# A depthwise convolution on GpSimd by two phases of tokens: 47 half-width taps in place of 62

## The chip, the cores and the metric

The kernel runs on one NeuronCore of a Trainium2 chip. TensorE (PE) multiplies matrices, VectorE (DVE), ScalarE (ACT) and GpSimd (POOL) work elementwise, and SyncE (SP) issues the DMAs between HBM and the on-chip memory SBUF. Every engine executes its own list of instructions in order; an instruction whose operands are not ready holds up everything behind it in its list. TensorE writes to PSUM, eight banks of 128x512 fp32 numbers. The metric is the device time of one execution in microseconds (us). Times are given as the median of several runs; the profile belongs to one more execution.

## The reference

One layer of a streaming encoder over 1088 tokens (1024 of a prompt, 64 of a sample), model width 1024, fp32:

```python
h = x + 0.5 * _swiglu(x, ffn1_norm, ffn1_w_in, ffn1_w_out)
u = _rms(h, mix_norm)
z = u @ w_in                      # q | k | v | q_idx | k_idx | w_idx | conv GLU in | gates
...                               # rotary, indexer scores, top-k keys per query, attention over them
c = ca * jax.nn.sigmoid(cb)
c_pad = jnp.concatenate([past_conv, c], axis=1)
dc = lax.conv_general_dilated(c_pad, conv_w[:, None, :], window_strides=(1,), padding='VALID',
                              feature_group_count=CONV_CH) + conv_b      # 31 taps, 512 channels
conv_out = jax.nn.silu(_layernorm(dc, conv_ln_g, conv_ln_b)) @ conv_w_out
g_a, g_c = jnp.split(jax.nn.sigmoid(gate + b_gate), 2, axis=-1)
merged = g_a * (attn @ attn_w_out) + g_c * conv_out
h = h + merged @ w_out
h = h + 0.5 * _swiglu(h, ffn2_norm, ffn2_w_in, ffn2_w_out)
```

The change concerns `dc` alone: every channel is filtered over time with its own 31 coefficients. With channels on the partitions, one tile of 128 channels is a row of 1148 numbers per partition (30 of padding, 1024 of the prompt, 30 of the sample's past, 64 of the sample), and it gives 1118 sums, output n being the bias plus the sum over j of w[j] * c[n + j].

## The kernel before

Activations stand channels by tokens; every large product is made of three fp32r matmuls (high and low parts of weights and activations), so a weight is loaded by SP as `raw`, rounded by ACT to `whi` (L118) and its rest `wlo` is made by POOL (L119). `raw` and `whi`/`wlo` have three buffers each. The order of every engine's list comes from a scheduler that simulates the program with its own costs and priorities; nothing is reordered at run time.

The stages are: feed-forward 1, the input projection with the convolution and the indexer (790 to 1204 us of the profile), attention with what is left of gates, convolution branch and merge (to about 1650 us), the output projection, feed-forward 2. In the stage that the change touches these things run side by side:

- **Projections on PE**, in chunks of 364 or 362 tokens. A chunk of one weight is 24 matmuls into one of four PSUM banks (`ps4`): conv GLU columns for tiles 0 and 3, keys, indexer queries, values, conv GLU columns for tiles 1 and 2 (`conv_in`), attention queries, and then twelve of the sixteen gate weights (`gates`, three chunks each). ACT takes each gate chunk out of PSUM with a Tanh into `sg` (L1138), and SP stores it (L1139).
- **The convolution** (`conv`). Tile 3 goes to DVE (L751). Tiles 0, 1 and 2 go to ACT and POOL: a tile is done in two halves of 559 outputs; ACT makes the first product with the bias (`ac`, L761) and then for each of 30 further taps a product `pd` = w[j] * c (L765); POOL adds it to `ac` (L766). There are two buffers of `pd`, so ACT can be two taps ahead of POOL, and one buffer each of the input `ci` and of `ac`. A half ends with the store of `ac` (L767).
- **The indexer and its top-k**: scores by PE (L919, L920), Relu on ACT (L921), weighted sums `Y` on DVE (L924, L926), a POOL memset of the causal corner (L929), and then a search of the 256th largest score per row: 15 rounds of counting (L989 on DVE, L979 on ACT for one tile), the low bits (L1018, L1020), the mask `bias` (L1054), and behind a branch on a value read by DVE the breaking of ties (L1106 to L1115), tile by tile in the order 5, 6, 4, 3, 2, 1, 0 with a flag tested for each.
- **The start of attention**: logits `lg` (L1185, L1186) into three new PSUM banks that lie over those of `ps4` and so wait until every gate chunk is out of them; DVE adds `bias` to `lg` (L1188), which waits for the whole search; ACT exponentiates (L1198). The other four gates and the layer norm of the convolution's output (`norm`, from L1274) are filled in between.

Of the kernel before, what the change touches and what calls it, by code (L numbers as in the profile page):

```python
# [9 lines left out]
F32 = mybir.dt.float32  # L10
# [5 lines left out]
AF = mybir.ActivationFunctionType  # L16
ALU = mybir.AluOpType
AX = mybir.AxisListType

P = 128  # L20
# [34 lines left out]
CW = 31  # L55
# [3 lines left out]
PAR = {}  # L59
# [33 lines left out]
class Kern:  # L93
# [349 lines left out]
    def ffn(self, h, s, offs, gp, tp, steps, tail, lead=(), ready=(), last=False, lp=None):  # L443
# [20 lines left out]
        if lead:  # L464
            run(ready)
# [60 lines left out]
    def run(self):  # L526
        tc, nc, a = self.tc, self.nc, self.a
        PS = bass.MemoryType.PSUM
        with ExitStack() as top:
# [6 lines left out]
            d_c = dram.tile([4, P, 1148], F32, name="d_c")  # L536
            d_dc = dram.tile([4, P, 1118], F32, name="d_dc")
# [12 lines left out]
            for n_, o_, w_ in (("bgate", 0, 16), ("lnb", 16, 4)):  # L550
                q0 = PAR[n_][0]
                nc.scalar.activation(hb[:, o_:o_ + w_], self.par[:, q0:q0 + w_], AF.Copy, scale=0.5)
            wq = cst.tile([P, 9, 8], F32, name="wq")

            def par(n, i=0):
                o = PAR[n][0] + i
                return self.par[:, o:o + 1]
# [175 lines left out]
            bias = bp.tile([P, BCOLS], BF16, name="bias")  # L733
            cvs = ExitStack()
            cvp_ = self.pool(cvs, "convp", 1, side="right")
            ep = self.pool(cvs, "evict", 1, side="right")
            low = ExitStack()
            kp = self.pool(low, "topk", 1, side="right")
# [2 lines left out]
            def conv(t, dve):  # L741
                x = "d" if dve else "p"
                if dve:
                    for s0, w in ((0, 374), (374, 372), (746, 372)):
                        ci = cvp_.tile([P, 589], F32, name="ci", tag="ci" + x)[:, :w + 30]
                        nc.sync.dma_start(ci, d_c[t, :, s0:s0 + w + 30])
                        ac = lgi.tile([P, 512], F32, name="acc", tag="lgi")[:, :w]
                        nc.scalar.activation(ac, ci[:, 0:w], AF.Identity, scale=par("convw", t * CW),
                                             bias=par("convb", t))
                        for j in range(1, CW):  # L750
                            nc.vector.scalar_tensor_tensor(ac, ci[:, j:j + w], par("convw", t * CW + j), ac,  # L751
                                                           op0=ALU.mult, op1=ALU.add)
                        co = cvp_.tile([P, 559], F32, name="ac", tag="ac" + x)[:, :w]
                        nc.scalar.activation(co, ac, AF.Copy)
                        nc.sync.dma_start(d_dc[t, :, s0:s0 + w], co)
                    return
                for s0 in (0, 559):
                    ci = cvp_.tile([P, 589], F32, name="ci", tag="ci" + x)
                    nc.sync.dma_start(ci, d_c[t, :, s0:s0 + 589])
                    ac = cvp_.tile([P, 559], F32, name="ac", tag="ac" + x)  # L760
                    nc.scalar.activation(ac, ci[:, 0:559], AF.Identity, scale=par("convw", t * CW),  # L761
                                         bias=par("convb", t))
                    for j in range(1, CW):
                        pd = cvp_.tile([P, 559], F32, name="pd", tag="pd", bufs=2)
                        nc.scalar.activation(pd, ci[:, j:j + 559], AF.Copy, scale=par("convw", t * CW + j))  # L765
                        nc.gpsimd.tensor_tensor(ac, ac, pd, op=ALU.add)  # L766
                    nc.sync.dma_start(d_dc[t, :, s0:s0 + 559], ac)  # L767

            def load_q(pool, src, t0, rows, qpool=None, qb=2, n=1280):

# [18 lines left out]

            conv_in(3, ep)  # L790
            conv(0, False)
            conv(3, True)
            tbs = ExitStack()
            kx = self.pool(tbs, "kidx", 1)
# [37 lines left out]
            for i in (0, 1):  # L832
                b = bias[:, BOFF[i]:BOFF[i] + ATILES[i][3]]
# [20 lines left out]
            def spare(n):  # L854
                rows, y0, L = rows_of(n)
                return bias[:rows, BOFF[n + 2]:BOFF[n + 2] + L]
# [51 lines left out]
            for n in SORD:  # L908
# [4 lines left out]
                for hd in range(8):  # L913
                    nb = 2 if L > 512 else 1
                    pw = L // nb
                    for b in range(nb):
                        o = lgi.tile([P, 512], F32, name="lgi", tag="lgi")[:rows, :pw]
# [33 lines left out]
            r2s.close()  # L951
            conv_in(1, ep)
            conv(1, False)
            conv_in(2, ep)
            conv(2, False)
# [102 lines left out]
            with tc.If(more > 0):  # L1058
# [40 lines left out]
                for n in (5, 6, 4, 3, 2, 1, 0):  # L1099
# [4 lines left out]
                    with tc.If(tied > 0):  # L1104
                        y, b = Y[:rows, y0:y0 + L], spare(n)
# [280 lines left out]
            def gate_part():  # L1386
                steps = gates(gorder[GPRE:], ak, 2)
                for _ in range(3 * (16 - GPRE) - 7):
                    next(steps)
                    yield  # L1390
                lp = C["pool"] = self.pool(cx, "ln", 1)
                yield from both(norm(2, lp, lp), steps)
                act_es.close()

            def conv_part():
                lp_ = C["pool"]
                with cx:
                    lq = self.pool(cx, "lnq", 1, side="right")
                    for c, q in ((2, lq), (1, lp_), (0, None)):
                        yield from both(conv_out(c, lq), norm(c - 1, lp_, q) if c else iter(()))  # L1400

            def merge_part():
                self.act = self.pool(ac_es, "act2", 2, side="right")
                self.mp = self.pool(mg_es, "merge", 1, side="right")
                yield from merge(2, self.mp)

            def wout_part():
                yield from wout(2, h_dram(self.mp))

            def last_part():  # L1410
                yield from merge(1, self.mp)
# [8 lines left out]
            parts = [gate_part(), conv_part(), merge_part(), wout_part(), last_part()]  # L1420
# [211 lines left out]
```

## Time and profile before

| | us |
|---|---|
| median of 3 runs | 2360.64 (2358.08 to 2363.79) |
| the profiled execution | 2364.21, its span 2362.4 |
| PE busy | 2254.3 (95% of the span) |
| POOL busy | 1557.9 (66%) |
| DVE busy | 1690.9 (72%) |
| ACT busy | 1416.6 (60%) |

Shares of the span are averages over stages with different limits. How to read what is shown below: a row of the timeline is start, duration, engine, source line, operation, output tile<-input tiles, shapes, count, and in brackets how long the engine was idle before it and what released it. A row of waits is the waiting instruction and what it waited for, with the total in us, the number of times and the longest. A row of the windows is a stretch of time, its length, and for PE, PEld (weight loads), DVE, ACT and POOL the busy time and the number of instructions, then the granted clock of TensorE (1.00 is full), the DMA share and GB/s.

### The profile page before, as it was taken

The page shows a single profiled execution, that of the slowest core. Times are in us where ns is not written, and L with a number is a line of the kernel's source. Part 1 is how long each engine was busy: PE and PEld are TensorE (multiplying, and loading weights), DVE is VectorE, ACT ScalarE, POOL GpSimd, SP SyncE. Part 2 cuts the span into 40 slices and gives each one's busy share as a digit, 9 for nine tenths or more (in the row PEclk, how much of TensorE's full clock was granted, in tenths as well). Part 3 has the DMA queues.
Part 4 walks back from the last instruction along what each step waited for, and adds up shares of the span by engine and source line. Part 5 has one row for each costly group of instructions (what it writes and reads, how often), then busy time and mean ns, then how long its engine had stood idle before and what let it go on. Part 6 is the DMA issues. An engine that isn't in the chain of part 4 may idle for free. (4 is left out here: it accounts for less than half of the span.)

```text
span 2362.4 us, 44344 instructions
## 1 busy us (share of the span) xinstructions
PE 2254.3 (95%) x16226; PEld 2216.6 (94%) x16226; DVE 1690.9 (72%) x3868; ACT 1416.6 (60%) x2926; POOL 1557.9 (66%) x1071
## 2 busy tenths in 40 slices
PE   7999999999999999999979998899999999999997
PEld 6999998999999999999978888799999999999997
DVE  7887766887767287689846777457877757887765
ACT  6655655656646546887456667447655555556553
POOL 5667755767657786889863544558667765667654
PEclk9999999999999999999989999999999999999999
DMA  5332323333334434234222446763333232333333
GB/s 187 107 107 91 108 93 116 99 99 99 99 99 135 138 127 135 85 105 134 85 84 73 149 143 180 224 214 108 99 99 102 88 121 68 110 112 103 99 99 110
DMA packets 130412, 273.45 MB, mean 116 GB/s; under 512 B 17936, under 2 KB 77200, under 8 KB 130192
## 3 DMA queue, kind: packets, MB, share of 16 engines
q1 hardware_dynamic: 130192, 270.61, 35.8%
q8 instruction: 127, 2.08, 0.4%
q14 instruction: 93, 0.76, 0.1%
HBM read 231.87 MB, written 38.75 MB: 115 GB/s over the span
## 5 line engine op out<-in xcount | busy, mean ns | idle before, releaser
L136 PE MATMUL ps<-x,wp 128*128 128x272 f32 x1760 | 508.5, 290 | 6.3 <-ACT wp L152 3.3
L138 PE MATMUL ps<-x,wp 128*128 128x272 f32 x1760 | 504.3, 291 | 4.4 <-POOL wp L153 2.6
L137 PE MATMUL ps<-x,wp 128*128 128x272 f32 x1760 | 506.5, 289 | 0.0
L136 PE MATMUL ps<-x,whi 128*128 128x272 f32 (+2 forms) x1544 | 482.6, 313 | 10.5 <-ACT sg L1138 3.6
L153 POOL TENSOR_TENSOR wp<-s,wp 128x512 fp32r<-128x512 f32 x272 | 363.9, 1349 | 190.0 <-ACT wp L152 185.9
L138 PE MATMUL ps<-x,wlo 128*128 128x272 f32 (+2 forms) x1544 | 480.8, 312 | 0.0
L327 POOL TENSOR_TENSOR wlo<-raw,whi 128x1024 fp32r<-128x1024 f32 x120 | 290.4, 2420 | 186.7 <-ACT whi L326 177.8
L137 PE MATMUL ps<-x,whi 128*128 128x272 f32 (+2 forms) x1334 | 412.1, 309 | 1.0 <-POOL x L153 1.0
L119 POOL TENSOR_TENSOR wlo<-raw,whi 128x1024 fp32r<-128x1024 f32 (+1 forms) x123 | 277.9, 2262 | 154.0 <-ACT whi L118 149.1
L136 PEld LDWEIGHTS ps<-x,wp 128*128 128x128 f32 x1760 | 331.3, 189 | 10.6 <-ACT wp L152 4.7
L138 PEld LDWEIGHTS ps<-x,wp 128*128 128x128 f32 x1760 | 328.5, 188 | 8.2 <-DVE wp L153 4.4
L137 PEld LDWEIGHTS ps<-x,wp 128*128 128x128 f32 x1760 | 332.0, 189 | 0.0
L136 PEld LDWEIGHTS ps<-x,whi 128*128 128x128 f32 x1544 | 292.8, 190 | 13.4 <-ACT sg L1138 3.9
L766 POOL TENSOR_TENSOR ac<-ac,pd 128x559 f32<-128x559 f32 x180 | 272.5, 1514 | 39.6 <-ACT ac L761 19.0
L138 PEld LDWEIGHTS ps<-x,wlo 128*128 128x128 f32 x1544 | 292.7, 190 | 1.0
L137 PEld LDWEIGHTS ps<-x,whi 128*128 128x128 f32 x1334 | 253.6, 190 | 2.3 <-POOL x L153 1.3
L152 ACT ACTIVATE wp<-s 128x512 fp32r<-128x512 f32 x272 | 167.8, 626 | 130.3 <-DVE s L314 80.6
L765 ACT ACTIVATE pd<-ci,par 128x559 f32<-128x559 f32 x180 | 135.7, 758 | 96.8 <-POOL ac L766 85.8
L152 ACT ACTIVATE wp<-ps 128x512 fp32r<-128x512 f32 x208 | 123.1, 592 | 113.1 <-DVE ps L312 100.2
L439 DVE SCALAR_TENSOR_TENSOR h<-ps,h 128x272 f32<-128x272 f32 x448 | 174.9, 431 | 13.1 <-PE ps L138 12.4
L326 ACT ACTIVATE whi<-raw 128x512 fp32r<-128x512 f32 x240 | 138.5, 624 | 74.5 <-DMA raw<-wf 70.4
L137 PE MATMUL ps<-gl,whi 128*128 128x272 f32 x640 | 182.7, 291 | 0.0
(278 smaller groups left out, 5934.0 us busy)
## 6 DMA issues: line engine op xcount, KB each, us to landing
raw<-wf SPq DMA_DIRECT2D x353, 512.0 KB, 3.4
d_g<-sg SPq DMA_DIRECT2D x32, 181.0 KB, 1.9
d_h<-h SPq DMA_DIRECT2D x2, 2176.0 KB, 10.3
y<-t SPq DMA_DIRECT2D x32, 136.0 KB, 1.8
raw<-wf SPq DMA_DIRECT2D x16, 256.0 KB, 2.7
raw<-d_q SPq DMA_DIRECT2D x32, 128.0 KB, 3.0
raw<-d_qi SPq DMA_DIRECT2D x24, 128.0 KB, 3.2
d_g<-sg SPq DMA_DIRECT2D x16, 182.0 KB, 2.9
```

The source lines that it names most:

```text
L119: self.weng.tensor_tensor(lo[:, :n], raw[:, :n], hi[:, :n], op=ALU.subtract)
L136: t.matmul(out, wh, xh, start=first, stop=False, skip_group_check=onto)
L137: t.matmul(out, wh, xl, start=False, stop=False, skip_group_check=onto)
L138: t.matmul(out, wl, xh, start=False, stop=last, skip_group_check=onto)
L152: nc.scalar.activation(hi, x, AF.Copy)
L153: (eng or nc.vector).tensor_tensor(lo, x, hi, op=ALU.subtract)
L326: self.nc.scalar.activation(hi[:, c], raw[:, c], AF.Copy)
L327: self.weng.tensor_tensor(lo, raw, hi, op=ALU.subtract)
L439: nc.vector.scalar_tensor_tensor(x, p, 0.5, x, op0=ALU.mult, op1=ALU.add)
L765: nc.scalar.activation(pd, ci[:, j:j + 559], AF.Copy, scale=par("convw", t * CW + j))
L766: nc.gpsimd.tensor_tensor(ac, ac, pd, op=ALU.add)
```

## The change

In place of two halves of 559 neighbouring outputs, a tile on ACT and POOL is now cut into even and odd outputs. The whole row of 1148 inputs is loaded at once; `even` and `odd` are views of it with every second number, and `both` (tile `cb`) is a POOL addition of the two, shifted. Three filters of half width run over them, with the 15 odd coefficients over `odd`, the 16 even ones over `even`, and 16 sums of neighbouring coefficients over `both` (`cvs2`, made once). With o, e and w their results, the even outputs are e + o and the odd ones w - o - e shifted by one; the biases (once in o, twice in w) come out right. So a tile has 15 + 16 + 16 = 47 products in place of 62, 44 additions of products in place of 60, and four further additions (one for `both`, three for the outputs, two of which write every second number). Two thirds of the products read every second fp32 number. The input row and the output row share two buffers (tag `cip`), `ac` has three, `pd` two as before. A tile is loaded by one DMA and stored by one, in place of two and two. DVE's tile is unchanged.

```diff
@@ run()
             cvp_ = self.pool(cvs, "convp", 1, side="right")
+            cvs2 = cvp_.tile([P, 4, 17], F32, name="cvs2")
+            q0 = PAR["convw"][0]
+            w31 = self.par[:, q0:q0 + 4 * CW].rearrange("p (t j) -> p t j", j=CW)
+            q0 = PAR["convb"][0]
+            nc.gpsimd.tensor_tensor(cvs2[:, :, 0:15], w31[:, :, 0:30:2], w31[:, :, 1:31:2], op=ALU.add)
+            nc.scalar.activation(cvs2[:, :, 15], w31[:, :, 30], AF.Copy)
+            nc.scalar.activation(cvs2[:, :, 16], self.par[:, q0:q0 + 4], AF.Copy, scale=2.0)
@@ conv(t, dve), the branch for ACT and POOL
-                for s0 in (0, 559):
-                    ci = cvp_.tile([P, 589], F32, name="ci", tag="ci" + x)
-                    nc.sync.dma_start(ci, d_c[t, :, s0:s0 + 589])
-                    ac = cvp_.tile([P, 559], F32, name="ac", tag="ac" + x)
-                    nc.scalar.activation(ac, ci[:, 0:559], AF.Identity, scale=par("convw", t * CW),
-                                         bias=par("convb", t))
-                    for j in range(1, CW):
-                        pd = cvp_.tile([P, 559], F32, name="pd", tag="pd", bufs=2)
-                        nc.scalar.activation(pd, ci[:, j:j + 559], AF.Copy, scale=par("convw", t * CW + j))
+                ci = cvp_.tile([P, 1150], F32, name="ci", tag="cip", bufs=2)
+                nc.sync.dma_start(ci[:, 0:1148], d_c[t])
+                nc.gpsimd.memset(ci[:, 1148:1150], 0.0)
+                even, odd = (ci.rearrange("p (m t) -> p m t", t=2)[:, :, i] for i in (0, 1))
+                both = cvp_.tile([P, 574], F32, name="cb", tag="cb")
+                nc.gpsimd.tensor_tensor(both, even[:, 1:575], odd[:, 0:574], op=ALU.add)
+                q0 = PAR["convw"][0] + t * CW
+                parts = ((odd, 559, par("convb", t), [self.par[:, q0 + 2 * i + 1:q0 + 2 * i + 2] for i in range(15)]),
+                         (even, 560, None, [self.par[:, q0 + 2 * i:q0 + 2 * i + 1] for i in range(16)]),
+                         (both, 559, cvs2[:, t, 16:17], [cvs2[:, t, i:i + 1] for i in range(16)]))
+                sums = []
+                for x, n, b, ws in parts:
+                    ac = cvp_.tile([P, 560], F32, name="ac", tag="acp", bufs=3)[:, :n]
+                    sums.append(ac)
+                    if b is None:
+                        nc.scalar.activation(ac, x[:, 0:n], AF.Copy, scale=ws[0])
+                    else:
+                        nc.scalar.activation(ac, x[:, 0:n], AF.Identity, scale=ws[0], bias=b)
+                    for j in range(1, len(ws)):
+                        pd = cvp_.tile([P, 560], F32, name="pd", tag="pd", bufs=2)[:, :n]
+                        nc.scalar.activation(pd, x[:, j:j + n], AF.Copy, scale=ws[j])
                         nc.gpsimd.tensor_tensor(ac, ac, pd, op=ALU.add)
-                    nc.sync.dma_start(d_dc[t, :, s0:s0 + 559], ac)
+                o, e, w_ = sums
+                out = cvp_.tile([P, 1150], F32, name="co", tag="cip", bufs=2)
+                oe, oo = (out[:, 0:1118].rearrange("p (m t) -> p m t", t=2)[:, :, i] for i in (0, 1))
+                nc.gpsimd.tensor_tensor(oe, e[:, 0:559], o, op=ALU.add)
+                nc.gpsimd.tensor_tensor(w_, w_, o, op=ALU.subtract)
+                nc.gpsimd.tensor_tensor(oo, w_, e[:, 1:560], op=ALU.subtract)
+                nc.sync.dma_start(d_dc[t], out[:, 0:1118])
```

The lines after the edit move by 24 (L1138 becomes L1162, L1185 becomes L1209); the tap's product and addition become L783 and L784. Since the scheduler makes the lists anew, other work moves too. Three places matter below.

**ACT, from the last products of the convolution to the first exponential.** Before (`pd` a tap's product, `sg` a gate chunk leaving PSUM, `pr` attention's exponentials):

```order
L765 ACTIVATE pd<-ci,par 128x559 x3
L118 ACTIVATE whi<-raw 128x1024
L1138 ACTIVATE sg<-ps,hb 128x362
L765 ACTIVATE pd<-ci,par 128x559 x2
L1138 ACTIVATE sg<-ps,hb 128x364
L1198 ACT_TABLE_LOAD
```

and now, where the convolution's last products stand:

```order
L783 ACTIVATE pd<-cb,cvs_10352 128x559 x2
L1162 ACTIVATE sg<-ps,hb 128x362
L783 ACTIVATE pd<-cb,cvs_10352 128x559 x2
L118 ACTIVATE whi<-raw 128x1024
L1162 ACTIVATE sg<-ps,hb 128x362
L1162 ACTIVATE sg<-ps,hb 128x364
L1162 ACTIVATE sg<-ps,hb 128x362
```

Before, the last gate chunk ahead of the logits (the 362 in the third row) has all but two of the convolution's products ahead of it in ACT's list. Now thirteen gate chunks stand between the last product and the logits' own instructions.

**POOL at the same place** (`wlo` a weight's rest, `ls` the layer norm's sums, `pr` attention's scaling). Before:

```order
L766 TENSOR_TENSOR ac<-ac,pd 128x559 x4
L1058 UNCONDITIONAL_BRANCH
L766 TENSOR_TENSOR ac<-ac,pd 128x559 x3
L119 TENSOR_TENSOR wlo<-raw,whi 128x1024
L766 TENSOR_TENSOR ac<-ac,pd 128x559 x6
L119 TENSOR_TENSOR wlo<-raw,whi 128x1024
L766 TENSOR_TENSOR ac<-ac,pd 128x559 x2
L1201 ISA
```

and now:

```order
L784 TENSOR_TENSOR ac<-ac,pd 128x559 x6
L119 TENSOR_TENSOR wlo<-raw,whi 128x1024
L789 TENSOR_TENSOR ac<-ac 128x559
L790 TENSOR_TENSOR co<-ac 128x559
L119 TENSOR_TENSOR wlo<-raw,whi 128x1024
L1299 TENSOR_TENSOR ls<-lx 128x784
L119 TENSOR_TENSOR wlo<-raw,whi 128x1024
L1082 UNCONDITIONAL_BRANCH
L119 TENSOR_TENSOR wlo<-raw,whi 128x1024 x2
L1225 ISA
```

The convolution's last addition moves from behind the branch to ahead of it, with four weights' rests and the layer norm's first sum after it.

**SP at the first tile** (`d_c` the convolution's input in HBM). Before:

```order
L711 DMA d_c<-sg 128x362
L759 DMA ci<-d_c 128x589
L117 DMA raw<-wf 128x1024
L713 DMA d_c<-sg 128x298
L714 DMA d_c<-sg 128x64
```

and now:

```order
L712 DMA d_c<-sg 128x298
L713 DMA d_c<-sg 128x64
L714 DMA co<-sg 128x30
L715 DMA co<-sg 128x30
L117 DMA raw<-wf 128x1024
L764 DMA ci<-d_c 128x1148
```

The load of a tile, which needed two of its three chunks, now stands behind the stores of all three.

## The prediction

> **What bounds the kernel now.** The page comes first. TensorE is busy for 95% of the span, so what counts is where it stands still, and the convolution is not PE work. Its groups on the page:
>
> ```profile
> L766 POOL TENSOR_TENSOR ac<-ac,pd 128x559 f32<-128x559 f32 x180 | 272.5, 1514 | 39.6 <-ACT ac L761 19.0
> L765 ACT ACTIVATE pd<-ci,par 128x559 f32<-128x559 f32 x180 | 135.7, 758 | 96.8 <-POOL ac L766 85.8
> ```
>
> An addition takes twice as long as the product that feeds it, and ACT waits 85.8 us for POOL to give a `pd` back. These waits stand in ACT's list, ahead of whatever is behind them. Next the windows, to see whether PE feels it (columns as above):
>
> ```profile
> 936.00:1163.00 227.00, 227.00 (x1365) 225.24 (x1364) 189.19 (x437) 168.41 (x303) 195.50 (x125) 1.00 0.35 107
> 1163.00:1204.00 41.00, 22.61 (x108) 21.44 (x107) 23.84 (x47) 17.97 (x26) 39.13 (x21) 0.75 0.22 71
> ```
>
> Until 1163 PE is never idle. In the 41 us up to the end of the convolution it works 22.6, POOL 39.1, and the clock falls to 0.75. PE's waits between 790 and 1210 us name the cause:
>
> ```profile
> PE lg L1185 <- ACT sg L1138: 14.8, 1, 14.8
> PE ps L136 <- ACT sg L1138: 3.6, 1, 3.6
> PE ps L136 <- DVE sg L709: 3.3, 1, 3.3
> ```
>
> PE waits for gate chunks to leave PSUM, 18.4 us in two pieces (the 3.3 are earlier, at 790). ACT, whose 0.54 us per chunk cannot be the trouble, does this at that time:
>
> ```profile
> 1195.24 0.76 ACT L765 ACTIVATE pd<-ci,par 128x559 f32<-128x559 f32 x1 [1.14 <-POOL ac L766]
> ...
> 1196.86 0.54 ACT L1138 ACTIVATE sg<-ps,hb 128x362 f32<-128x362 f32 x1
> 1197.30 1.59 ACT L765 ACTIVATE pd<-ci,par 128x559 f32<-128x559 f32 x2
> ```
>
> The last chunk leaves at 1197.4 behind products that wait for POOL. POOL's backlog thus decides when attention starts. PE's own rows give the loss:
>
> ```profile
> 1165.14 0.32 PE L138 MATMUL ps<-x,wlo 128*128 128x362 f32 x1
> 1169.09 0.67 PE L136 MATMUL ps<-x,whi 128*128 128x364 f32 x1 [3.63 <-ACT sg L1138]
> 1169.86 0.51 PE L138 MATMUL ps<-x,wlo 128*128 128x364 f32 x1
> 1170.16 0.51 PE L136 MATMUL ps<-x,whi 128*128 128x364 f32 x1
> ...
> 1182.36 0.32 PE L138 MATMUL ps<-x,wlo 128*128 128x362 f32 x1
> 1197.45 0.80 PE L1185 MATMUL lg<-kh,qt 128*128 128x512 f32 x1 [14.77 <-ACT sg L1138]
> ...
> 1204.71 0.39 PE L1185 MATMUL lg<-kh,qt 128*128 128x512 f32 x1
> 1204.94 0.40 PE L1186 MATMUL lg<-kl,qt 128*128 128x512 f32 x1
> ```
>
> After the first stop 11 matmuls start 0.30 us apart instead of 0.16: 1.5 us. Without stop and slow clock the last gate chunk would be done at 1182.5 - 3.8 - 1.5 = 1177.2. Then come six `lg` matmuls, 0.235 apart as in the last two rows: 1178.6. Then, in the new list, 25 matmuls of the next gate before the fourth logit pair (19 in the old one): 1182.8. In the old run that pair started at 1204.71. So **21.9 us** is all that PE can gain here; after it PE is full:
>
> ```profile
> 1210.00:1225.00 15.00, 15.00 (x89) 14.28 (x88) 6.66 (x21) 12.90 (x21) 12.74 (x5) 1.00 0.33 111
> 1225.00:1250.00 25.00, 25.00 (x180) 24.59 (x179) 13.55 (x36) 15.37 (x26) 7.73 (x3) 1.00 0.23 70
> ```
>
> **When POOL is done.** For tiles 1 and 2, by the groups of POOL between 945 and 1205:
>
> ```profile
> L766 POOL TENSOR_TENSOR ac<-ac,pd 128x559 f32<-128x559 f32 x117 | 182.8, 1562 | 24.6 <-ACT ac L761 12.0 <-ACT pd L765 5.9
> L119 POOL TENSOR_TENSOR wlo<-raw,whi 128x1024 fp32r<-128x1024 f32 x18 | 44.2, 2457 | 8.0 <-ACT whi L118 7.9
> ```
>
> Now each tile has 48 POOL operations (44 additions, one for `both`, three at the end). Two tiles at 1.56 us are 150 us, and the new list has 14 splits among them: 34 us. Tile 1 can start when its third chunk is stored and the whole row loaded:
>
> ```profile
> 940.70 0.53 DVE L709 SCALAR_TENSOR_TENSOR sg<-sg,ps 128x362 f32<-128x362 f32 x1 [0.33 <-ACT ps L706]
> ...
> d_c<-sg SPq DMA_DIRECT2D x4, 149.0 KB, 1.9
> ci<-d_c SPq DMA_DIRECT2D x6, 294.5 KB, 2.9
> lx<-d_dc SPq DMA_DIRECT2D x1, 784.0 KB, 4.9
> ```
>
> 941.2 + 1 of issuing + 1.9 for the store + some 4 for 574 KB (between the last two rows) is 948 to 949. With 5 us of waits (the old restarts on a single `ac` and `ci`, most of the 24.6, are gone) POOL ends at 949 + 150 + 34 + 5 = **1138**, 65 us before the old end. The last product leaves ACT some 8 us earlier, at 1130. The gate chunk behind it is the 24th of 36, and at PE's full pace (24 matmuls of 0.166, 4.0 us a chunk) it is ready at 1177.2 - 12 x 4.0 = 1129; with four banks PE would stop only after 1141. So PE reaches its logits unhindered: the stall of 18.4 us and its slow matmuls go. ACT's 39 fewer products are hidden; POOL's removal counts only through that stall.
>
> **What is late next.** The fourth logit pair needs a bank that DVE frees with its first L1188, and that stands behind the search:
>
> ```profile
> 1186.81 0.88 DVE L1106 TENSOR_SCALAR_CACHE_REDUCE Y<-Y,sth 128x640 f32<-128x640 f32 x1 [2.82 <-DVEq L1104]
> 1192.12 1.87 DVE L1115 SCALAR_TENSOR_TENSOR bias<-Y,bias 128x640 bf16<-128x640 f32 x1
> 1198.83 0.69 DVE L1188 CUSTOM_DVE_ANT_0 pr<-lg,bias 128x512 f32<-128x512 f32 x1 [4.84 <-PE lg L1186]
> ```
>
> The search ends at 1192.12 + 1.87 = 1194.0, and two flags and a jump follow; the 2.82 us covered four flags (tiles 6, 4, 3 and 2), 0.7 each, so I take 2.1: DVE was ready at 1196.1 (bounds 1194.0 and 1198.8). If DVE keeps its pace, the pair starts at 1196.8 in place of 1204.7, PE idles 14 us and pays the slow clock again (the old run lost 1.1 on six `lg` and 1.4 on eleven gate matmuls: 2.5). That is a gain of only 7.9 - 2.5 = 5.4.
>
> But DVE too is held by POOL's additions. Between 1143 and 1194 its operations with two SBUF inputs are stretched:
>
> ```profile
> L1108 DVE SCALAR_TENSOR_TENSOR need<-cnt,need 128x1 f32<-128x1 f32 x2 | 2.1, 1074 | 0.1
> 1133.97 0.17 DVE L1002 SCALAR_TENSOR_TENSOR srch<-flag,srch 128x6 f32<-128x6 f32 x1
> L1054 DVE SCALAR_TENSOR_TENSOR bias<-Y,sth,negc 128x896 bf16<-128x896 f32 x1 | 2.3, 2274 | 0.0
> L1054 DVE SCALAR_TENSOR_TENSOR bias<-Y,sth,negc 128x1024 bf16<-128x1024 f32 x1 | 1.3, 1328 | 0.0
> L1054 DVE SCALAR_TENSOR_TENSOR bias<-Y,sth,negc 64x192 bf16<-64x192 f32 x1 | 1.5, 1469 | 0.0
> L1113 DVE SCALAR_TENSOR_TENSOR Y<-rk,need,Y 128x1024 f32<-128x1024 f32 x1 | 2.2, 2196 | 0.0
> L1113 DVE SCALAR_TENSOR_TENSOR Y<-rk,need,Y 128x640 f32<-128x640 f32 x1 | 1.8, 1759 | 0.0
> L1018 DVE SCALAR_TENSOR_TENSOR bias<-Y,srch 128x1024 uint16<-128x1024 uint16 x1 | 1.9, 1904 | 0.0
> ```
>
> One column takes 1.07 us (L1108), where six took 0.17 in the second row: 0.9 each, twice. L1054 takes 1.33 for 1024 columns but 2.27 for 896 and 1.47 for 192: 1.1 too much, twice. L1113's two widths give 1.14 ns a column; that explains 1.17 of its 2.20 us, and L1054's undisturbed 1024 columns show only 0.16 over it, so 0.9 is waiting, in four such operations (L1113, L1115). L1018's seven lose some 1.7 in the same way (the longest 0.6). That is 1.8 + 2.2 + 3.6 + 1.7 = 9.3 us. Now POOL has no additions left there, only five splits of 2.4 in 51 us, so about a quarter stays: 7 us gained (bounds 4, if POOL ends late, and 9.3). Before that DVE waits for ACT's Relus behind the products:
>
> ```profile
> DVE Y L926 <- ACT lgi L921: 30.1, 37, 2.4
> ```
>
> By the new list 46 products stand among the Relus, 56 before: I take 2 us (bounds -3 and 5). DVE is ready at 1196.1 - 9 = 1187, the pair starts at 1187.8, PE idles 5.0 and loses some 2 to the clock.
>
> The Trainium skill (SBUF, "Who interferes with whom") says that a DVE instruction with two SBUF inputs and a GpSimd instruction that reads SBUF exclude each other for a whole instruction. The 1.07 us for one column agree; by that rule alone all two-input operations outside splits go free, within the 4 to 9.3 above.
>
> **The rest of the change.** The first tile waits for its third chunk: its first product moves from 790 to about 801, ACT holds conv_in's next evictions for 2 or 3 us, and four PSUM banks cover that: -1 (0 to -4). SP's store of a tile waits for POOL's last addition, and weight loads stand behind it; but such a load needs a `raw` buffer that only POOL's next split in the same list gives back, so POOL's pace holds both already: 0. `cvs2` and the memsets, once each: 0. Attention's reordered list: 0, with 3 either way.
>
> **The sum:** 21.9 - 5.0 - 2 - 1 = 13.9 us, taken as 14. The profiled run took 2364.21 with a span of 2362.4, 3.6 above the median; the difference is applied to the median: 2360.6 - 14 = **2346.5**.
>
> **The rivals.** *The search binds fully* (DVE gains nothing, since it waits mostly for PE and for its own chain): gain 5.4 - 1, time 2356. For it: DVE is busy 189 of 227 us. Against it: the stretched rows.
>
> *Everything goes*: DVE comes 15 us earlier and no stop is left, gain 20 to 22: 2339 to 2341. Against it: the search is one chain of rounds without idle time.
>
> *Nothing measurable*: the PE time won at 1200 is lost to waits of the reordered attention, whose PE idle (the page's slices 21 to 28) a new list can raise: 2356 to 2361.
>
> *Slower: strided products.* 93 of the 141 products read every second fp32 number, which no row shows. The nearest is ACT over every second 16-bit number, against a plain row of its width:
>
> ```profile
> 1013.44 1.15 ACT L979 ACTIVATE bias<-Y,cand 128x1024 bf16<-128x1024 uint16 x1 [0.46 <-DVE cand L901]
> 1030.04 1.05 ACT L118 ACTIVATE whi<-raw 128x1024 fp32r<-128x1024 f32 x1
> ```
>
> That is 10% at most; doubling is the other end. By the new list some 20 strided products stand among the Relus and rounds that ran from 1005 to 1050, where ACT had almost no idle time. At 0.76 more each the search starts 15 us late, POOL ends at 1177 and relieves DVE by 4 only: ready at 1207, 2 to 6 us slower than before, about 2365. It decides from 0.5 us more each. I take nothing, by the nearest row.
>
> The Trainium skill (GPSIMD Engine Reference, "Performance pitfalls") has POOL's reads slow down by half only beyond a byte step of 8, and the step here is 8; no run here shows it, and it says nothing of ACT.
>
> **How the numbers follow.** Forecast 57%, the search binds 14%, everything goes 8%, nothing 12%, slower 9%. This kernel's measurement tells 0.2%, 4.7 us, from no change. The forecast and "everything goes" are faster, and so is half of the second, whose time lies at that bound: 0.72; its other half and "nothing" are same: 0.19; slower 0.09. The forecast's own range, from DVE's bounds, is 2340 to 2354; with the tails 2337 to 2358.
>
> **What would show it.** Right: no PE wait on `sg`; POOL's last convolution operation near 1138 and ACT's products far ahead of the first exponential; L1108 below 0.5 us; the logits after DVE, not after ACT, with PE idle some 5 us. Wrong: a tap's product above 1.2 us; PE waiting for `sg` at 1130 to 1180; or DVE's first addition of `bias` to `lg` no earlier than 1196, which would mean that its chain did not move.

## The result, and the profile after

The changed kernel takes 2337.97 us (median of 6 runs, 2334.56 to 2339.77) beside 2359.39 for the kernel before (6 runs): a ratio of 0.9903, 95% interval 0.9892 to 0.9914, 21.4 us less where 14 were forecast. The profiled execution took 2337.39 with a span of 2335.6. Measured again on three chips, the ratio was 0.9904, 0.9913 and 0.9922; their mean with the first is 0.991, 21 us.

PE's waits of the changed kernel between 775 and 1210 us (waiting instruction, what it waited for, total, times, longest):

```profile
PE lg L1209 <- DVE mb L1212: 3.9, 1, 3.9
PE ps L136 <- DVE sg L708: 2.0, 1, 2.0
PE lg L1209 <- ACT sg L1162: 1.8, 1, 1.8
```

Of the 18.4 us on `sg` 1.8 are left, and the longest wait is now the one on DVE. The timeline of PE at the logits shows the same (start, duration, engine, line, operation, idle before):

```profile
1178.11 0.50 PE L1209 MATMUL lg<-kh,qt 128*128 128x512 f32 x1 [1.76 <-ACT sg L1162]
...
1187.79 0.79 PE L1209 MATMUL lg<-kh,qt 128*128 128x512 f32 x1 [3.86 <-DVE mb L1212]
```

The logits begin at 1178.1 in place of 1197.5, and the fourth pair at 1187.8 in place of 1204.7. The groups of POOL and ACT in that stretch, shapes kept apart (busy us, mean ns of one, idle before):

```profile
L784 POOL TENSOR_TENSOR ac<-ac,pd 128x559 f32<-128x559 f32 x87 | 126.5, 1454 | 18.9 <-ACT pd L783 14.2 <-ACT ac L780 0.3
L783 ACT ACTIVATE pd<-ci,par 128x559 f32<-128x559 f32 x42 | 33.3, 799 | 7.0 <-POOL ac L784 7.0
L783 ACT ACTIVATE pd<-cb,cvs 128x559 f32<-128x559 f32 x45 | 34.0, 758 | 23.8 <-POOL ac L784 23.7
L768 POOL TENSOR_TENSOR cb<-ci 128x574 f32<-128x574 f32 x3 | 3.4, 1139 | 11.4 <-DMA ci<-d_c 11.4
```

A product that reads every second number takes 799 ns, one over neighbouring numbers 758: 5% more. The windows show what became of the 41 us up to the old end of the convolution (PE, PEld, DVE, ACT and POOL busy, then the granted clock):

```profile
1163.00:1204.00 41.00, 35.38 (x187) 33.42 (x186) 22.35 (x59) 14.91 (x21) 10.22 (x4) 0.92 0.15 54
```

PE works 35.4 of them in place of 22.6, POOL 10.2 in place of 39.1. The last rows of DVE's search:

```profile
1171.53 0.16 DVE L1132 SCALAR_TENSOR_TENSOR need<-cnt,need 128x1 f32<-128x1 f32 x1
...
1182.56 0.89 DVE L1137 SCALAR_TENSOR_TENSOR Y<-rk,need,Y 128x640 f32<-128x640 f32 x1
1183.47 0.83 DVE L1139 SCALAR_TENSOR_TENSOR bias<-Y,bias 128x640 bf16<-128x640 f32 x1
1187.03 0.69 DVE L1212 CUSTOM_DVE_ANT_0 pr<-lg,bias 128x512 f32<-128x512 f32 x1 [2.73 <-DMA d_g<-sg]
```

The single column that took 1.07 us takes 0.16, the 640 columns of the last two operations 0.89 and 0.83 in place of 1.76 and 1.87, and the first addition of `bias` starts at 1187.0 in place of 1198.8.

### The profile page after: what moved, and what is told of

Its sections match the earlier page's. It is cut to its first block, busy times and chain, and to the rows that moved or that the text cites. A ratio compares the mean times of both kernels' runs of the same rounds, so it can differ in the third digit from the quotient of the medians.

```text
span 2335.6 us, 44194 instructions
## 1 busy us (share of the span) xinstructions
PE 2250.3 (96%) x16226; PEld 2213.6 (95%) x16226; DVE 1689.2 (72%) x3868; ACT 1390.8 (60%) x2883; POOL 1499.4 (64%) x1039
## 5 line engine op out<-in xcount | busy, mean ns | idle before, releaser
L784 POOL TENSOR_TENSOR ac<-ac,pd 128x559 f32<-128x559 f32 (+1 forms) x132 | 192.5, 1459 | 22.8 <-ACT pd L783 15.4
L137 PE MATMUL ps<-gl,wp 128*128 128x272 f32 x640 | 180.9, 288 | 0.0
L136 PE MATMUL ps<-gh,wp 128*128 128x272 f32 x640 | 178.8, 290 | 1.9 <-DVE h L439 1.8
```

What stands on the lines that cost most here:

```text
L136: t.matmul(out, wh, xh, start=first, stop=False, skip_group_check=onto)
L137: t.matmul(out, wh, xl, start=False, stop=False, skip_group_check=onto)
```

## Where the gain arises along the profile

The same points of PE's and DVE's work in the two profiles, in us from the start:

| | before | after | earlier by |
|---|---|---|---|
| start of the stage (second `sg<-sg,ps` of DVE) | 783.1 | 784.4 | -1.3 |
| fourth logit pair | 1204.7 | 1187.8 | 16.9 |
| first transposition of attention (`pt`) | 1218.3 | 1204.1 | 14.2 |
| last product with the values (`pv`) | 1526.0 | 1506.4 | 19.6 |
| last `ga` of the merge | 1589.7 | 1565.7 | 24.0 |
| end of the span | 2362.4 | 2335.6 | 26.8 |

The first row is none of the change's doing. Ahead of it the lists of PE, DVE and ACT are the same in both kernels (5813, 1310 and 1027 instructions), and yet the changed kernel reached this point at 784.4, 783.1, 779.8 and 782.9 us in its four profiles. Such a difference is of the execution and not of the change:

```profile
783.09 0.52 DVE L709 SCALAR_TENSOR_TENSOR sg<-sg,ps 128x362 f32<-128x362 f32 x1
```

```profile
784.40 0.52 DVE L708 SCALAR_TENSOR_TENSOR sg<-sg,ps 128x362 f32<-128x362 f32 x1
```

Counted from there, the gain in this pair is 18.2 us at the fourth logit pair and 15.5 at the first transposition, behind the matmuls that follow the stop at a slow clock. All profiles with these same lists up to the logits (four with the old lists, seven with the new) give 18.9 and 16.8 in the mean. So the start of attention (the junction, below) brings about 17 where 14 were forecast, and more came behind it, where the forecast had "0, with 3 either way". Part of the 26.8 is the profiled execution of the kernel before, 4.8 above its median. The experiments take the two apart: what makes the junction, and what the rest is.

Below, a ratio is to the kernel before on the same chip with its 95% interval (0.001 is 2.4 us); "from the stage" is the time from the start of the stage to the fourth logit pair, "behind" the time from that pair to the end of the span in the profile.

| kernel | ratio | 4th pair at | from the stage | behind |
|---|---|---|---|---|
| before (two profiles) | 1 | 1204.7, 1207.4 | 421.6, 422.8 | 1157.7, 1157.5 |
| after (four profiles) | 0.9903, 0.9904, 0.9913, 0.9922 | 1187.8, 1187.4, 1184.3, 1185.5 | 403.4, 404.3, 404.5, 402.6 | 1147.8, 1155.8, 1154.2, 1158.2 |
| before, 25 of 31 taps | 0.9944, 0.9941 (0.9928 to 0.9957) | 1187.9, 1190.0 | 405.0, 405.8 | 1156.0, 1157.0 |
| before, two buffers | 0.9954 (0.994 to 0.9968) | 1190.1 | 409.8 | 1156.9 |
| after, 60 additions | 0.9969 (0.9959 to 0.998) | 1197.0 | 412.9 | 1154.1 |
| after, 40 idle additions | 1.0011 (0.9999 to 1.0023) | 1226.1 | 442.1 | 1137.9 |
| after, 20 idle additions | 0.9954 (0.9939 to 0.9968) | 1195.8 | 411.2 | 1157.3 |
| after, no ties | 0.9894 (0.9877 to 0.991) | 1184.9 | 401.6 | 1150.9 |
| after, 13 gates first | 0.9895 (0.9878 to 0.9911) | 1196.9 | 411.4 | 1147.0 |
| after, three `pd` | 0.9918 (0.9902 to 0.9934) | 1191.4 | 405.7 | 1159.4 |
| before, `al` on POOL | 1.0008 (0.9999 to 1.0018) | 1207.8 | 421.5 | 1157.0 |
| after, `al` on POOL | 0.988 (0.9863 to 0.9897), 0.991 (0.9895 to 0.9924) | 1187.4, 1186.5 | 403.2, 402.2 | 1148.4, 1149.4 |
| before, rate 0.6 | 1.0013 (1.0001 to 1.0024) | 1206.7 | 422.5 | 1160.1 |
| after, rate 0.6 | 0.9945 (0.9924 to 0.9966) | 1186.3 | 402.4 | 1164.2 |

## Experiments on the junction

**Fewer taps, all else as before.**

```diff
-                    for j in range(1, CW):
+                    for j in range(1, 25):
```

> The kernel before, whose halves on GpSimd have only the first 25 of their 31 taps (six are left out, so the convolution's numbers are not the reference's): 48 additions per tile as the change has POOL operations, but with plain strides, two restarts per tile and one buffer. Theory (POOL's count of operations decides through ACT's list): in tiles 1 and 2, 24 additions of 1.56 us fall away, POOL ends at about 1203 - 37 = 1166, PE's wait for sg goes, and the logits wait for DVE: 2339 to 2343. Rival (the restarts on a single ci and ac, 24.6 us of POOL's waits, were as important): POOL still ends too late for the last gate chunks, 2348 or more.

Its ratio is 0.9944, 13 us, between the two expectations. The logits behave as the theory says: no stall on `sg`, fourth pair at 1187.9. But it stays short of the change, so it was run again beside it:

> The changed kernel again, beside the next three on one chip: 0.989 to 0.992 of the kernel before, as twice measured.

> The kernel before with 25 of the 31 taps on GpSimd (six left out), again. Its profile had the logits where the changed kernel has them (4th pair 1187.9) and no wait on ga in the merge, but its time was 14 below the kernel before instead of 21 to 24. If its list of attention is the worse one, it stays 5 us or more above the changed kernel on the same chip (ratio to before 0.993 to 0.995); if that was the chip, it equals it within 2 us.

0.9941 against 0.9913: 6 to 7 us above the changed kernel on one chip, with intervals that just touch. Counted from the start of the stage, the rounds of the search are done (the copy of `hibx` on DVE) at 350.9 us here and at 344.0 in the changed kernel beside it, but the fourth pair comes only 1.3 later (405.8 and 404.5). So little of the 6 to 7 us stands at the junction, and the number of additions is not quite all.

**Two buffers, all else as before.**

```diff
-                    ci = cvp_.tile([P, 589], F32, name="ci", tag="ci" + x)
+                    ci = cvp_.tile([P, 589], F32, name="ci", tag="ci" + x, bufs=2)
-                    ac = cvp_.tile([P, 559], F32, name="ac", tag="ac" + x)
+                    ac = cvp_.tile([P, 559], F32, name="ac", tag="ac" + x, bufs=2)
```

> The kernel before with two buffers for ci and for ac, all 62 taps. Theory (POOL's count decides): the restarts hide 10 to 20 us of POOL's waits, POOL ends at 1183 to 1193, still among the gate chunks and over the whole search: a gain of 3 to 8, 2351 to 2356. Rival (the restarts were the trouble): all of it, 2338 to 2342. Third: nothing, 2358 to 2361.

0.9954, 11 us: more than the theory allowed, with all 62 taps. PE's waits up to 1210 in this kernel:

```profile
PE lg L1185 <- ACT sg L1138: 7.2, 1, 7.2
PE lg L1185 <- DVE mb L1188: 3.4, 1, 3.4
```

The stall on `sg` is only partly gone. But the rounds of the search end 345.2 us from the start of the stage, where the kernel before has 351.1 and 353.0 and the changed kernel 342.2 to 344.0. ACT's waits between 945 and 1130 give a likely reason. First the kernel before, then the changed one:

```profile
ACT pd L765 <- POOL ac L766: 20.7, 25, 2.5
ACT pd L765 <- DMA ci<-d_c: 9.7, 3, 5.1
```

```profile
ACT pd L783 <- POOL ac L784: 23.5, 29, 3.0
ACT qt L801 <- DMA raw<-d_q: 3.5, 2, 3.1
```

The wait for POOL did not shrink in this stretch. What went is ACT's 9.7 us for the load of `ci` into its only buffer, which could not start before the half in it was done; the Relus that the search needs stood behind it in ACT's list. The kernel with fewer taps keeps the one buffer, shows that wait (4.3 and 3.5 us) and the late search; the one with two buffers shows neither. More buffers, which the change brings along, thus let the rounds end some 6 to 8 us earlier. That this goes by ACT's wait is argued and not shown: with fewer taps the wait is less than half as long and the search as late, and this run doubles `ac` as well as `ci`.

**The old number of additions in the changed kernel.**

```diff
-                    for j in range(1, len(ws)):
+                    for i in range(1, len(ws) + 4):
+                        j = i % len(ws)
```

> The changed kernel with four taps of every part used twice (the convolution's numbers are not the reference's): 60 products' worth of work on ACT and 56 additions + 4 per tile on POOL, as before, but with strides and buffers of the change. Theory (backlog on POOL): 24 more additions of 1.46 us in tiles 1 and 2, POOL ends at 1142 + 35 = 1177, DVE's search is stretched again, logits at about 1193: 2343 to 2348. Rival (the number of additions does not matter, the new list or the buffers do): 2336 to 2340. Third (the number is all): 2356 to 2360.

0.9969: 7 us are left of the gain. The rounds end early (340.5 us from the start of the stage), yet PE waits for `sg` again and the fourth pair starts at 1197.0:

```profile
PE lg L1210 <- ACT sg L1163: 10.4, 1, 10.4
```

So POOL's backlog does hold the gate chunks in ACT's list. It cost more than the theory's range, since POOL ended the convolution at 1191.5 and not at 1177.

**POOL busy with additions that nobody waits for.**

```diff
+                if t == 2:
+                    for _ in range(40):
+                        nc.gpsimd.tensor_tensor(both[:, 0:559], both[:, 0:559], sums[1][:, 0:559], op=ALU.add)
```

> The changed kernel with 40 more POOL additions behind the last tile (cb <- cb, ac), which no product feeds and nothing reads: ACT's list is as it was, POOL is busy with additions to about 1200. Theory (the additions hold DVE's operations with two SBUF inputs): L1132 takes about 1 us for one column again, the 4th logit pair starts at 1193 to 1196, and 4 to 8 us are lost: 2342 to 2346. Rival (the earlier search came from ACT's and PE's earlier work, not from POOL's silence): 2337 to 2339. Third (POOL's late splits and scalings hold PE too): above 2347.

1.0011: the whole gain is lost, for a reason that no theory had. DVE and POOL in this kernel:

```profile
1188.08 1.91 DVE L1142 SCALAR_TENSOR_TENSOR bias<-Y,bias 128x640 bf16<-128x640 f32 x1
1225.39 0.69 DVE L1215 CUSTOM_DVE_ANT_0 pr<-lg,bias 128x512 f32<-128x512 f32 x1 [35.41 <-DMA raw<-wf]
```

```profile
1152.94 13.43 POOL L794 TENSOR_TENSOR cb<-cb,ac 128x559 f32<-128x559 f32 x6
...
1196.46 11.53 POOL L794 TENSOR_TENSOR cb<-cb,ac 128x559 f32<-128x559 f32 x8
...
1222.56 2.80 POOL L794 TENSOR_TENSOR cb<-cb,ac 128x559 f32<-128x559 f32 x2
```

The search is done at 1190.0, but attention's first operation on DVE starts 0.03 us after POOL's last addition (1225.36). Attention's buffers take the place of the convolution's in SBUF, so the likely reason is that `pr` waits for `cb` to be given back (the row names a DMA instead). To separate this from the search, half the number was run:

> The changed kernel with 20 idle POOL additions in place of 40, so that POOL gives back the buffers of the convolution at about 1189, before attention writes over them. Theory (the additions hold DVE's search by the 5 to 6 us that 40 of them showed: 1184.3 to 1190.0): 4th logit pair at 1192 to 1194, 4 to 7 us above the changed kernel. Rival (attention gives that back): within 2 us of it.

0.9954 against 0.9913 beside it: 9.3 us by the medians, over the expected 4 to 7. DVE's last rows here:

```profile
1171.22 1.28 DVE L1133 TENSOR_SCALAR_CACHE_REDUCE Y<-Y,sth 128x1024 f32<-128x1024 f32 x1 [4.74 <-issue]
1172.54 0.83 DVE L1135 SCALAR_TENSOR_TENSOR need<-cnt,need 128x1 f32<-128x1 f32 x1
...
1188.37 1.87 DVE L1142 SCALAR_TENSOR_TENSOR bias<-Y,bias 128x640 bf16<-128x640 f32 x1
1195.03 0.69 DVE L1215 CUSTOM_DVE_ANT_0 pr<-lg,bias 128x512 f32<-128x512 f32 x1 [4.79 <-DMA d_g<-sg]
```

The breaking of ties takes 1171.2 to 1190.2, 19.0 us, and without POOL's additions 14.1 (1170.2 to 1184.3 in the changed kernel): 5 us through additions alone. DVE's list is the same in both. The other profiles agree: 19.2 and 19.4 us in the kernel before, 13.8 to 14.1 in all of the changed one, 13.4 with fewer taps, 19.6 with 40 idle additions. The Trainium skill (SBUF, "Who interferes with whom") says that a DVE instruction with two SBUF inputs and a GpSimd instruction that reads SBUF exclude each other; the row of one column agrees, 0.83 us with additions beside it and 0.16 without. Another 2 us lie between the search and the first addition of `bias` (4.79 idle, 2.73 in the changed kernel); what they are is open. The search's lateness goes into the time in full here: from the start of the stage the fourth pair comes 7 to 9 us later than in the changed kernel's four profiles (411.2).

**Taking the search off the junction.** First without the breaking of ties, then with a filler ahead of the logits:

```diff
-                for n in (5, 6, 4, 3, 2, 1, 0):
+                for n in ():
```

> The changed kernel without the breaking of ties (the loop of flags and L1130 to L1139 is left out; rows with ties keep too many keys). DVE is ready some 20 us earlier, at about 1166. Theory (the search still ends last at the junction): the 4th logit pair starts at 1183 to 1184 with no wait, PE's 3.9 us and some 2 us of slow clock go: 2331 to 2334. Rival (the stop at 1184 is given back later anyway, since attention has idle time on PE): 2336 to 2339.

```diff
-GPRE = 12
+GPRE = 13
```

> The changed kernel with 13 instead of 12 gate weights ahead of attention (GPRE), 12 us more of PE work that needs nothing from the search. Theory (PE idles for DVE at the junction and attention has enough other work to fill in): PE does not wait at the logits, 4 to 6 us gained: 2332 to 2334. Rival (the three chunks are missed as filling in attention): 2338 to 2344.

In both PE no longer waits for `mb` at the logits. Yet the ratios are 0.9894 and 0.9895, beside 0.9904 for the changed kernel on that chip: 2 us, within the intervals. The profile without ties starts its first transposition at 1198.5 (changed kernel 1202.5), 4 us earlier as the theory says, and ends at 2335.8 (2343.2), but its other runs stand near the changed kernel's. The rivals of both fit these times better than the theory, but four runs each leave some 5 us either way: whether those 4 us are given back later stays open.

**Three buffers for the products.** `bufs=2` of `pd` becomes 3.

> The changed kernel with three buffers for the products pd: ACT may be three taps ahead, so POOL waits less for products (15.4 us now) and ends its convolution up to 10 us earlier, at 1133 to 1142. Theory (the search is freed from more additions): 4th logit pair 1 to 3 us earlier, 0 to 3 us gained. Rival (ACT's Relus now stand behind more products, the search starts later): 0 to 5 us lost.

0.9918, no gain. POOL ended the convolution at 1133.2, but the rounds of the search end 347.5 us from the start of the stage, some 4 later than in the changed kernel, and the fourth pair 1 to 3 later: the rival's order of events. The loss in time (0.9918 against 0.9913 and the mean of 0.991) is small and not clear of the intervals.

## Experiments on what lies behind the junction

Two more profiles of the unchanged kernels came first:

> The kernel before once more, for a second profile. From the 4th logit pair to the end the first profile took 1157.7 us, 9.9 more than the changed kernel's 1147.8. If the new list makes attention and merge faster, the second profile shows 1155 or more; if the first was only a slow execution (4.8 above the median), 1151 to 1153.

> The changed kernel once more, for a second profile: from the 4th logit pair to the end 1147 to 1149 as in the first, if this part is steady; 1151 or more if it is chance.

Behind the fourth pair the kernel before is steady (1157.7, 1157.5), the changed one is not (1147.8, 1155.8, and 1154.2 and 1158.2 in the two further profiles). Part of the 26.8 was a fortunate execution of the changed kernel. The windows tell where. Each pair of rows is the stretch from the first transposition to the last product with the values, and from there to the end of the last `ga`: the kernel before, then the first and the second profile of the changed kernel.

```profile
1218.30:1526.40 308.10, 281.04 (x1798) 267.36 (x1796) 200.94 (x555) 201.35 (x417) 148.20 (x83) 0.95 0.47 143
1526.40:1590.20 63.80, 58.61 (x349) 58.16 (x349) 30.86 (x73) 24.32 (x42) 32.99 (x15) 0.97 0.73 245
```

```profile
1204.10:1507.20 303.10, 276.47 (x1791) 262.32 (x1789) 202.65 (x560) 202.00 (x417) 151.59 (x84) 0.97 0.49 149
1507.20:1566.20 59.00, 58.11 (x348) 58.12 (x349) 27.13 (x69) 22.74 (x39) 30.69 (x14) 0.97 0.73 245
```

```profile
1202.50:1512.10 309.60, 282.53 (x1791) 268.66 (x1789) 201.18 (x560) 201.99 (x417) 151.83 (x84) 0.94 0.49 145
1512.10:1572.90 60.80, 59.61 (x350) 59.12 (x349) 27.55 (x69) 22.84 (x39) 30.61 (x14) 0.95 0.73 240
```

In attention the two profiles of the changed kernel differ by 6.5 us, although their lists are the same and PE stands still about as long (26.6 and 27.1 us). The same matmuls took longer, with a granted clock of 0.94 in place of 0.97. The other two profiles of it (307.9 and 310.3 us at 0.95 and 0.94) are like the second, so attention itself is not faster than before. The second stretch is: 59.0 to 60.8 us in all four profiles, 63.8 and 64.1 before.

**The wait in the merge.** The kernel before has one clear stop there, from DVE's order. PE, then DVE:

```profile
1531.40 0.64 PE L136 MATMUL ps<-xh,whi 128*128 128x362 f32 x1 [5.05 <-DVE ga L1349]
```

```profile
1527.58 2.33 DVE L153 TENSOR_TENSOR al<-ar,ah 128x364 fp32r<-128x364 f32 x1 [1.55 <-issue]
...
1530.72 0.53 DVE L1349 SCALAR_TENSOR_TENSOR ga<-mpt,ps 128x362 f32<-128x362 f32 x1
```

A split of the next chunk stands ahead of the `ga` that frees PE's bank. The two-buffer kernel (4.7 us) and the one with 60 additions (5.1) have this stop too; the changed kernel and the one with fewer taps do not. Moving those splits away tests what it is worth:

```diff
-                    self.split(ah[:, k, :], al[:, k, :], ar, nc.gpsimd if k % 2 else nc.vector)
+                    self.split(ah[:, k, :], al[:, k, :], ar, nc.gpsimd)
```

> The kernel before with all splits al <- ar, ah of the merge on POOL instead of half of them on DVE; nothing ahead of attention is touched. Theory (in the old list DVE's al split stands ahead of the last ga operations, waits for its row and holds a PSUM bank: PE stands 5.1 us at 1526): that wait goes, 3 to 6 us gained (ratio 0.9975 to 0.9985), junction as before. Rival (the wait only moves, to POOL's splits or to PE's next wait): within 2 us of before.

1.0008: nothing, so the rival holds. The stop on `ga` falls to 3.0 us at most, and other waits grow (`ah` from 1.9 to 3.5 us). The 4 us that the merge gains (59.9 us for the second stretch above) are lost in attention ahead of it (311.3). A stop that a profile shows need not be worth its length.

In the changed kernel the same edit does more:

> The changed kernel with all splits of the merge's rows (al <- ar, ah) on POOL. The changed kernel's list has no 5 us wait on ga, so nothing is to be had there. Theory (list effects of either sign, some us): within 3 of the changed kernel, 0.989 to 0.993 of the kernel before. Rival (the splits on DVE still hold PE in the merge): 3 to 6 faster than the changed kernel, 0.988 or less.

> The changed kernel beside e18: 0.990 to 0.992 of the kernel before.

> The changed kernel with all splits of the merge's rows on POOL, again: 0.987 to 0.989 of the kernel before and 4 to 8 us below e17, if the first measurement was the list's doing; within 2 us of e17 if it was the chip's.

0.988 alone, and 0.991 against 0.9922 side by side: 2340.12 against 2344.18 us. It was the fastest kernel both times, but beside the changed kernel its lead of 4 us is not outside the intervals.

**The same lists in both kernels.** With 0.6 pieces filled in per slot of attention, the lists up to the logits stay as they are in each kernel, and those behind become almost the same in both: from the first logits on, 33 of PE's 8088 instructions stand elsewhere (285 without the edit), at most 9 on DVE (156) and 3 on ACT (96).

```diff
-RATE = (0.5, 1.0, 1.0, 0.5, 1.0)
+RATE = (0.6, 1.0, 1.0, 0.5, 1.0)
```

> The changed kernel with 0.6 instead of 0.5 pieces of the remaining gates and layer norm filled in per slot of attention; the lists up to the logits are the same, all later ones are new. 4th logit pair at 1184 to 1188 as before. Theory (the list of attention and merge is worth some us by itself): its time leaves 0.991 by more than 0.0012 in one direction. Rival (the later part is set by the same work whatever the list): 0.990 to 0.992.

> The kernel before with the same 0.6: junction as in the kernel before (4th pair 1205 to 1208), new lists behind it. Theory (its old list was a poor one, with the 5 us wait on ga): 3 to 6 us faster, 0.9975 to 0.9985. Rival: within 2 us of before.

0.9945 and 1.0013: both measure slower than with their own lists, the second by little more than its interval. PE's waits from 1210 to 1600, first of the changed kernel, then of the one before:

```profile
PE pt L1236 <- DVE pl L153: 11.2, 9, 3.1
PE ps L136 <- DVE ga L1373: 5.8, 4, 2.0
PE pv L1256 <- DVE oh L1263: 3.5, 3, 1.7
```

```profile
PE pt L1212 <- DVE pl L153: 11.2, 8, 3.3
PE ps L136 <- DVE ga L1349: 5.5, 4, 2.0
PE pv L1232 <- DVE oh L1239: 3.2, 2, 1.7
```

With equal lists behind, these waits are nearly equal and the change is worth 0.9945 / 1.0013 = 0.9932, 16 us (16.3 between the spans, 2366.8 and 2350.5; the two intervals together leave about 6 either way). That is the junction by itself, and the 16.8 us at the first transposition agree with it. And changed kernels with the same lists up to the logits (402.2 to 404.5 us from the stage to the fourth pair) lie between 0.988 and 0.9945 with their lists behind it: intervals 0.9863 to 0.9897 and 0.9924 to 0.9966 on one chip, 15 us between the middles and at least 6 between the ends.

## Why the prediction was right, and where not

**The stall on `sg`: right.** POOL ended the convolution at 1142.6 (1138 forecast), tile 1 started at 947.1 (948 to 949), PE reached the logits at 1178.1 (1177.2). The fewer-taps kernel shows that fewer additions suffice for this, the one with 60 additions that more buffers alone do not. (ACT has 45 products fewer, 62 to 47 in three tiles, and not 39; no term rests on it.)

**DVE's search is late next: right in place and time.** DVE's first addition of `bias` came at 1187.03 (1187 forecast), the fourth pair at 1187.79 (1187.8), PE's wait there 3.9 us (5.0). That it is right to a tenth is luck: the other three profiles have the pair at 1184.3 to 1187.4.

**But its sum of 7 and 2 came near by two errors that cancel.** The 2 us for fewer products among the Relus (bounds -3 and 5) were 8 in this pair, from the start of the stage to the end of the rounds (351.1 and 342.9): the step missed the second buffer, which is worth 6 to 8 us in the two-buffer kernel. The prediction used the restarts for POOL's end and not for ACT's list. The 7 us of relief from POOL's additions (bounds 4 and 9.3) were 59.8 - 57.0 = 2.8 from the end of the rounds to the end of the search. The breaking of ties gained the 5 us that the 20 idle additions give back, but the search, now earlier, met the end of the convolution and POOL's splits in the steps before it, and lost there again:

```profile
1136.40 3.25 DVE L1042 SCALAR_TENSOR_TENSOR bias<-Y,srch 128x768 uint16<-128x768 uint16 x1
...
1153.43 3.36 DVE L1078 SCALAR_TENSOR_TENSOR bias<-Y,sth,negc 128x896 bf16<-128x896 f32 x1
```

These 768 columns had taken 1.02 and the 896 columns 2.27. Together that is 11 us where 9 were forecast.

**The start, "-1 (0 to -4)": wrong in sign.** PE's wait at 790 fell from 3.3 to 2.0 us, a gain of 1.3. So this step was off by 2.3 us, about what the junction brought beyond the forecast: 15.5 us at the first transposition in this pair and 16.8 in the mean, where 13.9 stood.

**"Attention's reordered list: 0, with 3 either way": the step that failed.** No row was given for the 0 or for the 3, and the range of 2340 to 2354 was then made from DVE's bounds alone; the measured 2338 lies beyond it. The runs show that this term can be far larger: with the junction fixed, lists behind it moved the time by 15 us. With equal lists the change is worth 16 us, near the forecast 14; the measured 21 hold some 5 more, which is left for its own new list, though the intervals do not set this part apart from nothing. What is steady of it stands at the end of the merge, where the stop on `ga` is gone: 3 to 5 us in all four profiles. That this stop is the cause is not shown, since taking it away in the kernel before gave nothing, and the profiles of one and the same list scatter by 10 us behind the fourth pair.

**The rivals.** "The search binds fully" fell with DVE's earlier start; "nothing measurable" and "slower" did not occur: strided products cost 799 against 758 ns, where 0.5 us more would have been needed. "Everything goes" gave the nearest time (2339 to 2341), by another way than it said: PE's stop at the logits stayed.

## What to carry to other kernels

Where one list feeds several consumers, look at everything that stands ahead in it, reloads of a single buffer too: at the fourth pair more buffers alone gained 12 us and fewer additions alone 17, where the change with both gains 19, so the two overlap and neither has a share of its own. When a scheduler remakes the lists, allow for as much from the part that was not touched as from the effect under study (15 and 16 us here), and compare versions whose lists behind the change are alike. Count times in a profile from a point that the change cannot move, and not from the start of the span: here that start moved such a point by up to 5 us. A stop that the profile shows need not be worth its length, since the next wait can take it up.

## What the runs showed of the hardware

ACT reads every second fp32 number at 5% more (799 against 758 ns for 559 columns); POOL adds two such inputs without any loss that shows (`cb`, 574 columns, 1.14 us, where an addition of 559 neighbouring numbers takes 1.40 in the median). The Trainium skill (GPSIMD Engine Reference, "Performance pitfalls") expects a slowdown only beyond a byte step of 8, which these rows, at 8, agree with. DVE and POOL slow each other: in the kernel with 40 idle additions these took 2.24 us each beside the search (six in 13.43) and 1.44 where DVE stood waiting (eight in 11.53).
